# Moving small pieces of a tuned decoder trunk: first loads, three operands of the first SwiGLU, one raw sum, and the order of the last tiles

## The chip, the cores and the metric

The kernel runs on one core of a Trainium2 chip. Its time is the device time of one launch in microseconds (us); lower is better. The engines are named as in the profile: PE (TensorE, the matmuls, with PEld for its weight loads), DVE (VectorE), ACT (ScalarE), POOL (GpSimd) and SP (SyncE, which here only issues DMAs).

## The reference

Two layers over 512 tokens of width 1024, all in float32. Each layer is a SwiGLU block, a mixer (attention and a short convolution side by side) and a second SwiGLU block; a last RMSNorm ends it.

```python
def swiglu(h, w_gate, w_up, w_down):
    return (jax.nn.silu(h @ w_gate) * (h @ w_up)) @ w_down

for l in range(DEPTH):                       # DEPTH = 2, D_MODEL = 1024, D_FF = 2816
    x = x + 0.5 * swiglu(rms_norm(x, ffn1_norm[l]), ffn1_wg[l], ffn1_wu[l], ffn1_wd[l])
    h = rms_norm(x, mix_norm[l])
    z = h @ w_in[l]
    ...                                      # attention over 128 tokens, short convolution
    x = x + jnp.concatenate([attn_out, conv_out], axis=-1) @ w_out[l]
    x = x + 0.5 * swiglu(rms_norm(x, ffn2_norm[l]), ffn2_wg[l], ffn2_wu[l], ffn2_wd[l])
return rms_norm(x, final_norm)
```

## The kernel before

**Products.** Each float32 operand is split into a high part in fp32r and the rest (hi = cast on ACT, lo = raw - hi on DVE; `split`, L226), and a product takes three matmuls: hi x hi, hi x lo, lo x hi. Weights arrive as raw tiles of 512 KB (`load`, L209; eight buffers) and become `wh` and `wl`, three buffers each; `take_split` (L296) prepares them two groups ahead of PE.

**Seven products.** Most matrix products are done by a scheme of seven products in place of eight. The sums of the weights (`FORMS`: a11, a12, s2, s3, s1, a22, s4, each in two halves h = 0 and 1) are made partly by DMAs that accumulate (issued by POOL, L221: s1 and s3) and partly on DVE: s2 is the raw sum a11 + s1 (L265), made just before its split, and s4 is a12 + s2 (L285). The operands from the activations (`CHAINS`: b11, b21, t2, t3, t1, t4, b22) are made by `Seven.make`: t2, t1 and t4 need DVE subtractions or additions (L589 to L594), and all are split. In `winograd2` a loop over these seven steps streams one operand against one weight sum; steps are counted from 1 in the texts, so t2 is step 3, t1 step 5, t4 step 6, b22 step 7. A step is 24 matmuls of 128x512. After step n + 1 (n = 0, 1, 2) the operand of step n + 5 is made. The operands of a norm are made once and used by all its blocks, so this happens in the first block of a SwiGLU alone. Blocks are b = 1, 3, 5, 7, 9; b = 1 is the first, b = 3 the second.

**Order.** A planner (the tile framework) orders the instructions of each engine from its own costs; `tc.issue_after(ins)` puts what is traced inside it behind `ins` on that engine. Each engine then takes its instructions in that order. `state["rest"]` is the last lo split on DVE that was traced.

**Opening.** `x` comes token-major. `load_x(tp, c0, n)` loads columns c0 to c0 + n - 1 (of 128) of token half tp; `turn_x(c)` turns column tile c by four PE transposes, two from each token half, so it needs both halves' loads. `norm.take(c)` scales the turned tile into `xh` (ACT, L458) and `xl` (DVE, L459); `own` splits parts of the first three weight tiles, `go` multiplies them. `spin(n)` runs n matmuls on zeros. Order of the loads before: on ACT's queue x(0,1), then x(0,2) with x(0,3); on SP's queue x(0,0), x(1,0), half of the first weights, x(1,1), x(1,2) with x(1,3), the other half, and the rest.

**End.** The last seven-product block writes token-major. `close` adds a product to the output tile (DVE, L1318) and sums its squares (ACT, L1320); `guess` takes the reciprocal root (ACT, L1324) and `mend` refines it by one Newton step on DVE (L1329 for the mean, then three in `newton`, L433 to L435). `scale` multiplies half of the tile on DVE (L1364) and half on ACT (L1368) and issues the output DMA. The third token tile's product comes first, then the fourth's in two halves of 256 columns (`z_0`, `z_1`); in this section ACT and DVE run in the order in which the program is written.

## Time and profile before

| | |
|---|---|
| median of 3 runs | 1630.61 us (1630.34 to 1632.09) |
| the profiled execution | 1632.9 us, span 1631.1 us |
| PE busy | 1616.7 us, 99% of the span, 7572 matmuls |
| DVE busy | 1368.8 us, 84% |
| ACT busy | 1178.1 us, 72% |
| POOL busy | 223.6 us, 14% |
| granted PE clock, mean | 0.999 |

The span runs from the first instruction to the last; the rest of the execution's time lies around it. A row of the timeline gives the start in us from the start of the span, the duration, the engine (with q: its queue, which issues or waits), the line, the operation, the tile written and the tiles read, shapes and the count; in brackets the idle time of the engine before it and what ended it. A row of the waits gives the total, the times and the longest. A row of the critical chain gives start and length.

### The profile page before, as it was taken

The numbers are of one execution on the slowest core, as the hardware profiler recorded it, in microseconds if no ns is written. First come the engines' busy times: TensorE is split into PE (matmuls) and PEld (weight loads), VectorE is DVE, ScalarE is ACT, GpSimd is POOL, SyncE is SP. The second block draws the span as 40 slices with busy tenths as digits, with TensorE's granted clock in tenths as the row PEclk, the third lists the DMA queues.
The fourth block names the chain that finished last, engine by engine and source line by source line (L and its number), as shares of the span: only waits on it lengthen the run. The fifth ranks groups of instructions, "written<-read, shape, count | busy, mean of one in ns | idle before, by whom it ended". The sixth has DMA issues, their size and how long they took to land.

```text
span 1631.1 us, 21176 instructions
## 1 busy us (share of the span) xinstructions
PE 1616.7 (99%) x7572; PEld 1348.1 (83%) x7572; DVE 1368.8 (84%) x1779; ACT 1178.1 (72%) x1510; POOL 223.6 (14%) x199
## 2 busy tenths in 40 slices
PE   9999999999999999999999999999999999999998
PEld 6788888878898888888888888888788988888887
DVE  7978797888899977797999777989788998677997
ACT  6667777867766577778865777787586767878665
POOL 1211111001121111111011111110012111111121
PEclk9999999999999999999999999999999999999999
DMA  9899989922597698999967999999135978999992
GB/s 271 198 237 212 210 210 239 242 68 73 129 238 180 178 217 213 214 213 247 228 143 188 217 215 219 214 237 221 52 91 152 233 152 215 225 220 231 240 250 71
DMA packets 307166, 318.12 MB, mean 195 GB/s; under 512 B 125612, under 2 KB 188660, under 8 KB 307060
## 3 DMA queue, kind: packets, MB, share of 16 engines
q1 hardware_dynamic: 265140, 230.63, 49.9%
q0 software_dynamic: 41200, 85.47, 30.5%
q8 instruction: 59, 0.97, 0.2%
q10 hardware_dynamic: 720, 0.66, 0.1%
q14 instruction: 47, 0.39, 0.1%
HBM read 264.29 MB, written 2.10 MB: 163 GB/s over the span
## 4 chain that ended last, share of the span: by engine, by line
PE 91%; DVE 5%; ACT 2%; DMA 1%; issue 1%; SPq 0%; ACTq 0%; DVEq 0%
PE x L824 26%; PE y L824 13%; PE x_s L824 9%; PE w L824 6%; PE acc L313 6%; PE acc L312 6%; PE acc L315 6%; PE y_s L824 5%; PE w_s L824 3%; PE x_m L809 3%; PE y_m L809 1%; DVE wl L226 1%; PE y_e L824 1%; PE acc L686 1%; PE x_e L824 1%
## 5 line engine op out<-in xcount | busy, mean ns | idle before, releaser
L226 DVE TENSOR_TENSOR wl<-raw,wh 128x1024 fp32r<-128x1024 f32 (+1 forms) x493 | 599.6, 1224 | 171.8 <-ACT wh L226 171.0
L226 ACT CAST wh<-raw 128x1024 fp32r<-128x1024 f32 (+1 forms) x493 | 513.9, 1046 | 302.2 <-PE x L824 95.0
L313 PE MATMUL acc<-xl,wh 128*128 128x512 f32 x392 | 153.6, 392 | 2.8 <-DVE xl L459 2.8
L312 PE MATMUL acc<-xh,wh 128*128 128x512 f32 x392 | 153.4, 393 | 0.5 <-ACT wh L226 0.5
L315 PE MATMUL acc<-xh,wl 128*128 128x512 f32 x384 | 149.6, 390 | 0.0
L221 POOL DMA_DIRECT2D raw<-in_ffn_wu_dram x40 | 50.2, 1264 | 386.1 <-DVE wl L226 203.8
L313 PEld LDWEIGHTS acc<-xl,wh 128*128 128x128 f32 x392 | 73.7, 188 | 18.7 <-DVE xl L459 4.4
L312 PEld LDWEIGHTS acc<-xh,wh 128*128 128x128 f32 x392 | 73.7, 188 | 15.5 <-ACT wh L226 0.6
L315 PEld LDWEIGHTS acc<-xh,wl 128*128 128x128 f32 x384 | 72.1, 188 | 15.0
L221 POOL DMA_DIRECT2D raw<-in_ffn_wg_dram x40 | 49.4, 1261 | 200.9 <-DMA raw<-in_ffn_wu_dram 82.9
L221 POOL DMA_DIRECT2D raw<-in_ffn_wd_dram x34 | 41.0, 1206 | 246.3 <-DMA raw<-in_ffn_wd_dram 109.7
L265 DVE TENSOR_TENSOR raw<-raw,raw 128x1024 f32<-128x1024 f32 x58 | 70.6, 1221 | 3.6 <-DMA raw<-in_ffn_wu_dram 3.2
L1086 ACT COPY raw_a<-turned 128x1024 uint16<-128x1024 uint16 x48 | 63.5, 1357 | 0.0
L824 PE MATMUL x<-wl,ft2h 128*128 128x512 f32 x160 | 62.2, 390 | 1.1 <-DVE wl L226 1.1
L824 PE MATMUL y<-wh,ft4h 128*128 128x512 f32 x160 | 62.4, 390 | 0.1
L824 PE MATMUL w<-wh,fb21h 128*128 128x512 f32 x160 | 62.3, 390 | 0.0
L824 PE MATMUL y<-wh,ft3h 128*128 128x512 f32 x160 | 62.3, 390 | 0.0
L824 PE MATMUL w<-wl,fb21h 128*128 128x512 f32 x160 | 62.3, 389 | 0.0
L824 PE MATMUL x<-wh,ft2h 128*128 128x512 f32 x160 | 62.3, 389 | 0.0
L824 PE MATMUL x<-wh,ft1h 128*128 128x512 f32 x160 | 62.3, 389 | 0.0
L824 PE MATMUL x<-wh,ft2l 128*128 128x512 f32 x160 | 62.3, 389 | 0.0
L824 PE MATMUL x<-wh,ft1l 128*128 128x512 f32 x160 | 62.3, 389 | 0.0
(506 smaller groups left out, 4545.2 us busy)
## 6 DMA issues: line engine op xcount, KB each, us to landing
raw<-in_ffn_wu_dram SPq DMA_DIRECT2D x127, 512.0 KB, 5.4
raw<-in_ffn_wd_dram SPq DMA_DIRECT2D x105, 512.0 KB, 5.8
raw<-in_ffn_wg_dram SPq DMA_DIRECT2D x86, 512.0 KB, 5.3
raw<-in_ffn_wu_dram POOLq DMA_DIRECT2D x40, 512.0 KB, 8.9
raw<-in_ffn_wg_dram POOLq DMA_DIRECT2D x40, 512.0 KB, 6.2
raw<-in_w_in_dram SPq DMA_DIRECT2D x36, 512.0 KB, 4.0
raw<-in_ffn_wd_dram POOLq DMA_DIRECT2D x34, 512.0 KB, 9.4
raw<-raw POOLq DMA_DIRECT2D x21, 512.0 KB, 7.9
```

The lines of the kernel that those rows point to most:

```text
L221: nc.gpsimd.dma_start(out=r, in_=rows_of(*more), accum_op=ALU.add)
L226: return nc.scalar.copy(hi, raw), eng.tensor_sub(lo, raw, f32(hi))
L265: nc.vector.tensor_add(a11, a11, s1)
L312: nc.tensor.matmul(acc, hi[:, k, :], rhs[k][0], start=k == first, stop=False)
L313: nc.tensor.matmul(acc, hi[:, k, :], rhs[k][1], start=False, stop=False)
L315: nc.tensor.matmul(acc, lo[:, k, :], rhs[k][0], start=False, stop=k == last)
L686: nc.tensor.matmul(opening[n], (lo if part == "w" else hi)[:, k, :], xl if part == "x" else xh, start=n not in begun, stop=k == KC - 1 and ...
L809: nc.tensor.matmul(accs[c // 2][:, c % 2, :], w[:, k, cols], x_[:, 2 * h + k, :], start=start and c % 2 == 0 and h + k + i == 0, stop=h + ...
L824: nc.tensor.matmul(accs[u], x_[:, 2 * h + k, tok], w[:, k, :], start=start and h + k + i == 0, stop=h + k == 2 and i == 2, skip_group_chec ...
L1086: nc.scalar.copy(words(raws[self.b][:, c, :]), self.to[:, :, c, :])
```

## The change

1. The loads of x(1,1) and of x(0,2) with x(0,3) change queues and places. Two of the spins before the first transposes are left out.
2. In the first norm's SwiGLU (`norm.i == 0`) the operands of steps 5, 6 and 7 are made after steps 2, 3 and 4 instead of 1, 2 and 3, and their DVE instructions are put behind the last lo split traced by then.
3. In the first layer's first SwiGLU, block b = 3, the raw sum for the second half of s2 is put behind the lo split of the first half of a12 ("mark", "behind").
4. At the end `close` and `mend` are taken apart (`total` and `squared`, `mean` and `mend`), and the additions of the fourth token tile's two halves are written ahead of the scaling and of the small steps that wait for squares. The last Newton step takes two DVE instructions after the root instead of three, with one new small product ahead of it.

```diff
--- before.py
+++ after.py
@@ -261,6 +261,8 @@
                     late = state["late"] if h else None
                     if not state["late"] and how == "share":
                         late = state["rest"]
+                    if how == "behind":
+                        late = state["mark"]
                     with tc.issue_after(late) if late else nullcontext():
                         nc.vector.tensor_add(a11, a11, s1)
                 raw = {"a11": a11, "a12": a12, "s2": a11, "s3": s3, "s1": s1, "a22": a22, "s4": a12}[what]
@@ -271,6 +273,8 @@
                 sent = split_far(hi, lo, raw)
             else:
                 state["cast"], state["rest"] = (i.ins for i in split(hi, lo, raw))
+                if isinstance(order[n][1], tuple) and order[n][1][2] == "mark":
+                    state["mark"] = state["rest"]
             if isinstance(order[n][1], tuple) and order[n][1][0] == "end":
                 if what == "a12":
                     nc.gpsimd.dma_start(out=raw_of[raws["a11"]], in_=raw, accum_op=ALU.add)
@@ -383,7 +387,11 @@
                 if what == "w":
                     seven(
                         lambda o, j, h: ((wg, wu)[o], KC // 2 * j + 2 * h, 2, 2 * b * P, S),
-                        lambda what, h: "far" if (b, what, h) == (1, "a11", 0) else None,
+                        lambda what, h: "far"
+                        if (b, what, h) == (1, "a11", 0)
+                        else {("a12", 0): "mark", ("s2", 1): "behind"}.get((what, h))
+                        if near and b == 3
+                        else None,
                     )
                 if what == "s":
                     seven(
@@ -627,8 +635,8 @@
     load_x(1, 0, 1)
     load_x(0, 1, 1, nc.scalar)
     load(r0, 0, 0, 2)
-    load_x(0, 2, 2, nc.scalar)
-    load_x(1, 1, 1)
+    load_x(1, 1, 1, nc.scalar)
+    load_x(0, 2, 2)
     warm = small("warm", 1)
     nc.vector.memset(warm, 0.0)
     nc.scalar.activation(warm, warm, AF.Abs_reciprocal_sqrt, bias=eps)
@@ -716,7 +724,6 @@
     with tc.manual_schedule(engines={pe, act, dve}):
         spin(3)
         turn_rows(0)
-        spin(2)
         turn_x(0)
         own(0, 0, 2)
         norm.take(0, tps[0])
@@ -1015,8 +1022,10 @@
                             nc.scalar.activation(gates[2 + u], out, AF.Silu)
                             nc.vector.tensor_mul(ups[2 + u], ups[2 + u], gates[2 + u])
                 turns(step)
-                if step < 3:
-                    norm.make(CHAINS[step + 4][1])
+                due = step + (4 if norm.i else 3)
+                if 3 < due < len(CHAINS):
+                    with nullcontext() if norm.i else tc.issue_after(state["rest"]):
+                        norm.make(CHAINS[due][1])
                 if between:
                     between(step)
             if b in blocks:
@@ -1311,28 +1320,40 @@
             part = self.y[t][o]
             nc.vector.scalar_tensor_tensor(part, acc, by, part, op0=ALU.mult, op1=ALU.add)
 
+        def total(self, acc, t, half, by, c0=0):
+
+            y = self.y[t][half][:, c0 : c0 + acc.shape[1]]
+            nc.vector.scalar_tensor_tensor(y, acc, by, y, op0=ALU.mult, op1=ALU.add)
+            return y
+
+        def squared(self, y, ssq, name):
+
+            sq = work.tile([P, S], F32, tag="nsq", bufs=2, name=f"ysq_{name}")
+            nc.scalar.activation(sq[:, : y.shape[1]], y, AF.Square, accum_out=ssq)
+
         def close(self, acc, t, half, by, ssq, c0=0):
 
-            wide = acc.shape[1]
-            y = self.y[t][half][:, c0 : c0 + wide]
-            nc.vector.scalar_tensor_tensor(y, acc, by, y, op0=ALU.mult, op1=ALU.add)
-            sq = work.tile([P, S], F32, tag="nsq", bufs=2, name=f"ysq_{half}_{t}_{c0}")
-            nc.scalar.activation(sq[:, :wide], y, AF.Square, accum_out=ssq)
+            self.squared(self.total(acc, t, half, by, c0), ssq, f"{half}_{t}_{c0}")
 
         def guess(self, t, ssq, rest):
             r = small(f"r_end{t}", 1)
             nc.scalar.activation(r, ssq, AF.Abs_reciprocal_sqrt, scale=1.0 / D, bias=rest)
             return r
 
-        def mend(self, t, ssq, rest, r):
-            v, y = (small(f"{n}_end{t}", 1) for n in "vy")
+        def mean(self, t, ssq, rest):
+            v = small(f"v_end{t}", 1)
             nc.vector.scalar_tensor_tensor(v, ssq, 1.0 / D, rest, op0=ALU.mult, op1=ALU.add)
+            return v
+
+        def mend(self, t, v, r):
+            y = small(f"y_end{t}", 1)
             newton(y, r, v)
             return y
 
         def root(self, t, ssq, rest):
 
-            return self.mend(t, ssq, rest, self.guess(t, ssq, rest))
+            early = self.guess(t, ssq, rest)
+            return self.mend(t, self.mean(t, ssq, rest), early)
 
         def last(self, ops, accs):
 
@@ -1428,16 +1449,26 @@
             with tc.manual_schedule(engines={act, dve}):
                 ssq = piece(products(accs["x"][0], 0, 0, S, False), a, 0, 0.5)
                 early = self.guess(a, ssq, done[:, a : a + 1])
-                by = self.mend(a, ssq, done[:, a : a + 1], early)
+                v = self.mean(a, ssq, done[:, a : a + 1])
+                one = self.total(products(psum("mm", [P, H], "z_0"), 1, 0, H, True), b, 0, 0.5)
+                by = self.mend(a, v, early)
+                ssq = small("ssq_end_0", 1)
+                self.squared(one, ssq, "one")
                 for late in (0, 1):
                     scale(a, by, late)
-                one = piece(products(psum("mm", [P, H], "z_0"), 1, 0, H, True), b, 0, 0.5)
+                two = self.total(products(psum("mm", [P, H], "z_1"), 1, H, H, True), b, 0, 0.5, H)
                 rest = done[:, b : b + 1]
                 nc.vector.scalar_tensor_tensor(
-                    rest, one, 1.0 / D, rest, op0=ALU.mult, op1=ALU.add
+                    rest, ssq, 1.0 / D, rest, op0=ALU.mult, op1=ALU.add
                 )
-                two = piece(products(psum("mm", [P, H], "z_1"), 1, H, H, True), b, 0, 0.5, H)
-                by = self.mend(b, two, rest, self.guess(b, two, rest))
+                half = small("half", 1)
+                nc.vector.tensor_scalar_mul(half, rest, -0.5)
+                ssq, v, by = (small(f"{n}_last", 1) for n in ("ssq", "v", "y"))
+                self.squared(two, ssq, "two")
+                r = self.guess(b, ssq, rest)
+                nc.vector.scalar_tensor_tensor(v, ssq, -0.5 / D, half, op0=ALU.mult, op1=ALU.add)
+                nc.vector.tensor_scalar(v, v, r, r, op0=ALU.mult, op1=ALU.mult)
+                nc.vector.scalar_tensor_tensor(by, v, 1.5, r, op0=ALU.add, op1=ALU.mult)
                 for late in (1, 0):
                     scale(b, by, late)
```

## The prediction

> **What bounds the kernel now.** I read the page first, then the waits of the matmul engine, then the timeline at each place that the diff touches, and the critical chain there.
>
> ```profile
> span 1631.1 us, 21176 instructions
> PE 1616.7 (99%) x7572; PEld 1348.1 (83%) x7572; DVE 1368.8 (84%) x1779; ACT 1178.1 (72%) x1510; POOL 223.6 (14%) x199
> ```
> ```profile
> PE acc L313 <- DVE xl L459: 2.8, 4, 1.1
> PE xt L652 <- DMA xin<-in_x_dram: 1.6, 1, 1.6
> PE x L824 <- DVE wl L226: 1.1, 1, 1.1
> ```
>
> PE is busy 99% of the span. No matmul is added or removed except two spins, so the change can gain only where PE waits, and in the tail after its last matmul. The second view says how little that is: the three longest waits. The first (2.8) sits at the starts of the mixers, which the diff does not touch. The second is the opening, the third the first seven-product SwiGLU block. So the stakes are a few us of 1631; slower can come only from new waits.
>
> The profiled execution took 1632.9 us, 1.8 around the span; the median shown is 1630.61, or 2.3 less. I take the savings off the median. Differences under 0.2% (3.26 us) are about what a measurement of this kernel cannot tell from none.
>
> **Part 1, the opening.** Token tile 1 is turned from two loads; its second half, x(1,1), is what PE waits for.
>
> ```profile
> 1.21 0.98 ACTq L618 DMA_DIRECT2D xin<-in_x_dram  x2
> ```
> ```profile
> 2.30 4.59 DMA xin<-in_x_dram
> 11.45 3.24 PE acc L686 x13
> ```
> ```profile
> 1.19 2.74 PE L151 MATMUL idle<-zero 128*128 128x512 bf16 x6 [1.19 <-DVE warm L633]
> 4.08 0.61 PE L151 MATMUL idle<-zero 128*128 128x512 bf16 x2
> 6.93 0.44 PE L652 MATMUL xt<-ident,xin 128*128 128x128 f32 x2 [1.58 <-DMA xin<-in_x_dram]
> ```
> ```profile
> 5.64 0.40 ACT L226 CAST wh<-raw 128x256 fp32r<-128x256 f32 x1 [1.28 <-DMA raw<-in_ffn_wg_dram]
> 7.41 0.69 ACT L458 ACTIVATE xh<-xt,par 128x512 fp32r<-128x512 f32 x1 [0.78 <-PE xt L652]
> 8.46 0.42 ACT L226 CAST wh<-raw 128x256 fp32r<-128x256 f32 x1
> 9.92 0.69 ACT L458 ACTIVATE xh<-xt,par 128x512 fp32r<-128x512 f32 x1 [0.45 <-PE xt L652]
> ```
> ```profile
> DMA to landing us min/median/max: 4.6/4.7/4.9
> ```
>
> The first two fences show the exchange: x(1,1) is issued at 2.30 on SP's queue and lands at 6.89 (2.30 + 4.59, the chain's piece); x(0,2) with x(0,3) is the second of ACT's two, issued in the second half of their 0.98, about 1.7. They change places, so x(1,1) is issued 0.6 earlier and no longer behind 256 KB. It should land between 6.3 (0.6 earlier) and 5.6, where the first weights, issued beside it, have landed for the cast at 5.64. I take 5.6. ACT then goes from the first xh (ends 6.63) straight into the second (7.41): the 0.78 idle is gone. It does not all survive. The next cast, at 8.46, needs the second half of the first weights, issued at 3.33; the last row is the landing time of the two loads issued from 3.3 to 3.8, so 3.33 + 4.6 = 7.9. The bytes issued before it are the same, so the cast starts near 7.96: 0.50 gained, and the two xh behind it, the second of which (9.92) waits for PE, follow by 0.4 to 0.5. From 11.45 the chain is PE alone, so I carry **0.45** on. Ends: a loss of 0.15 (x(0,2) is issued 0.6 later and tile 2 waits for it: 0.45 less 0.6) and a gain of 1.2 (the weights come early too, so both the 0.78 and the 0.45 that ACT idles before the fourth xh go).
>
> The two spins (0.61) stood between a transpose group and a wait of 1.58 for data: free to remove, the cast at 5.64 waits for a DMA all the same.
>
> **Part 2, operands a step later.** In the first seven-product block VectorE is full. The first row is the busy time of the engines from 45 to 58 us, of 13.00 (PE, PEld, DVE, ACT, POOL, then the granted clock).
>
> ```profile
> 45.00:58.00 13.00, 12.12 (x54) 9.60 (x52) 13.00 (x12) 8.92 (x12) 3.69 (x5) 1.00 1.05 190
> ```
> ```profile
> 54.65 1.22 DVE L226 TENSOR_TENSOR ft1l<-hf,ft1h 128x1024 fp32r<-128x1024 f32 x1
> 56.92 1.22 DVE L226 TENSOR_TENSOR wl<-raw,wh 128x1024 fp32r<-128x1024 f32 x1
> 68.33 3.49 DVE L226 TENSOR_TENSOR wl<-raw,wh 128x1024 fp32r<-128x1024 f32 x3
> ```
> ```profile
> 96.08 5.44 PE x L824 x24
> ```
> ```profile
> 56.73 0.39 PE L824 MATMUL x<-wh,ft2l 128*128 128x512 f32 x1
> 58.19 0.50 PE L824 MATMUL x<-wl,ft2h 128*128 128x512 f32 x1 [1.07 <-DVE wl L226]
> 58.53 0.39 PE L824 MATMUL x<-wh,ft2h 128*128 128x512 f32 x1
> 68.98 0.39 PE L824 MATMUL x<-wh,ft1l 128*128 128x512 f32 x1
> 69.42 0.50 PE L824 MATMUL y<-wh,ft4h 128*128 128x512 f32 x1
> ```
>
> Step 3 (operand t2) runs four matmuls with wh, the last at 56.73, and gets its first wl at 58.14 (56.92 + 1.22). Undisturbed matmuls start 0.227 apart (the chain's 24 in 5.44), so it began near 56.04; 56.73 to 58.19 loses 1.23, and the next start, 0.34 on, another 0.11. Ahead of that wl stand the subtraction for t1 (L592) and ft1l, which step 5 needs only when it starts (four matmuls to 68.98, so 68.30). With the change they queue behind the last wl of s2. VectorE starts one every 1.14 (three in 3.49, the last taking 1.22), so two fewer bring the wl from 56.92 to about 54.7 (ScalarE's cast for it follows the raw sum at once), done at 55.9, before 56.5, when the third matmul wants it. That stall of 1.34 goes.
>
> What is late next is step 5. Its PE start moves from 68.30 to 66.96, so its first wl (68.33, the first of three) is wanted at 67.4. Of the work ahead of it fb22l (b22's) moves behind, now after s1's wl: done at 68.41 instead of 69.55. If ft4l, which now comes after s3's wl, falls behind as well, 67.27. So PE would be short by 0 to 1.0. Before, it was short by 1.25 and lost 0.32 (68.98 to 69.42 is 0.21 too long, and a restart of 0.11), because matmuls of the same and the next step were run in the gap. I take 0.2 lost where 0.32 was. ACT's three casts move along and issue no DMA. Part 2: 1.34 + 0.12 = **1.45**; ends 0.66 (1.0 paid where 0.32 was) and 1.66 (no stall left).
>
> **Part 3, the raw sum a part later.** The second block is where those gains could be taken back.
>
> ```profile
> 83.33 1.23 DVE L265 TENSOR_TENSOR raw<-raw,raw 128x1024 f32<-128x1024 f32 x1 [0.55 <-DMA raw<-in_ffn_wu_dram]
> 84.47 1.22 DVE L226 TENSOR_TENSOR wl<-raw,wh 128x1024 fp32r<-128x1024 f32 x1
> 87.78 1.23 DVE L265 TENSOR_TENSOR raw<-raw,raw 128x1024 f32<-128x1024 f32 x1 [1.49 <-DMA raw<-in_ffn_wu_dram]
> 89.53 1.22 DVE L226 TENSOR_TENSOR wl<-raw,wh 128x1024 fp32r<-128x1024 f32 x1
> ```
> ```profile
> 88.17 0.39 PE L824 MATMUL x<-wl,fb11h 128*128 128x512 f32 x1
> 90.88 0.42 PE L824 MATMUL w<-wl,fb21h 128*128 128x512 f32 x1
> ```
>
> VectorE takes its instructions in turn. The second raw sum waits 1.49 for an accumulating load, and queued behind it are a gate product and the wl at 89.53, done at 90.75; PE uses it at 90.88. So 0.13 of slack: the wait is just hidden. If PE comes 1.9 earlier (parts 1 and 2) and the load does not move, that order costs PE 1.8, nearly everything. With the change the sum stands behind this wl, which then follows its own cast, paced by PE's release of a buffer. The sum is wanted a step and a half (5.44 us each) later. So part 3 gains nothing by itself and keeps the gain: **0**. The first sum (83.33) is not moved; the wl behind it ends at 85.69, wanted at 88.17 now and 86.3 after: 0.6 of slack if its load stays where it is.
>
> **Part 4, the last tiles.**
>
> ```profile
> 1623.91 0.28 PE L1415 MATMUL z<-wl,fb_e 128*128 128x256 f32 x1
> 1623.04 0.75 DVE L1364 SCALAR_TENSOR_TENSOR ytok<-ytok,y_end,gain 128x512 f32<-128x512 f32 x1
> 1624.70 0.16 DVE L1436 SCALAR_TENSOR_TENSOR done<-ssq_end,done 128x1 f32<-128x1 f32 x1 [0.57 <-ACT ysq L1320]
> 1624.78 0.42 DVE L1318 SCALAR_TENSOR_TENSOR ytok<-z,ytok 128x256 f32<-128x256 f32 x1
> 1626.29 0.16 DVE L434 SCALAR_TENSOR_TENSOR v_end<-v_end,y_end 128x1 f32<-128x1 f32 x1
> 1626.49 0.16 DVE L435 SCALAR_TENSOR_TENSOR y_end<-v_end,r_end 128x1 f32<-128x1 f32 x1
> ```
>
> PE ends at 1624.19, but the last addition (L1318) starts at 1624.78: it stands behind L1436, which waits for the square of the first half. That came late because its addition stood behind the scaling at 1623.04. Now both additions go ahead, and the last can start near 1624.23: 0.55 earlier. After the root there are two small VectorE steps instead of three; one costs 0.19 (1626.29 to 1626.49). The new product with -0.5 (0.16) falls into the time of ScalarE's square. Sum **0.74**; ends 0.5 (the new order holds the last addition a little) and 0.8. The output DMA behind it is as before.
>
> **The sum.** 0.45 + 1.45 + 0 + 0.74 = 2.64: the profiled 1632.9 would be 1630.3, the median 1630.61 becomes 1628.0, 0.16% less. Ends of the parts together: 1.0 to 3.66, so 1629.6 to 1626.9.
>
> **Rivals.**
>
> *The opening gives its upper end.* If the weights land earlier together with x(1,1), ACT's two idle stretches go: 1.2 + 1.45 + 0.74 = 3.4, 1627.2, faster by just over 0.2%. For: the loads that share the queues change places. Against: no bytes go away. Chance 0.25.
>
> *The clock stays low.* Six spins took 2.74 (0.42 from start to start), the two later ones 0.61 (0.23): the clock rose at about 4. Without those two PE is emptier between 4 and 7; were it at half speed after that, each matmul that does not wait for anything else would cost 0.2 more, and as many as the chain's 13 from 11.45 would cost 2.6: no gain left, 1630.6. Against: it idled 1.58 before 6.93 and ran at 0.23 after. [...] Chance 0.05.
>
> *The new bound is step 5.* The full 1.0 is paid and x(0,2) is late: 1.0 gained, 1629.6. Chance 0.12.
>
> *Slower.* The first raw sum of the second block, still ahead of its wl, waits for a load that accumulates on the POOL queue.
>
> ```profile
> 74.69 1.21 POOL L221 DMA_DIRECT2D raw<-in_ffn_wu_dram  x1 [24.45 <-DVE wl L226]
> DMA to landing us min/median/max: 5.8/8.6/13.2
> ```
>
> That one was issued at 74.69 and landed by 83.3, 8.6 us; between 60 and 240 us such loads took 5.8 to 13.2. At 13.2 it lands 4.6 later; less 0.6 of slack PE stalls 4.0, and the kernel ends at 1632.0. It decides from a landing about 3.2 later than now, where the 2.64 are used up. For: the changed order moves the buffers' releases and so when these loads start and what they meet. Against: VectorE releases earlier, not later. Chance 0.10, most of it near the edge; with other new waits of the kind it holds the chance of slower by over 0.2%.
>
> **How the numbers follow.** The forecast holds 0.48, the rivals 0.25, 0.05, 0.12 and 0.10. Faster by over 0.2% is the first rival and the forecast's fast end: 0.31. Slower by over 0.2%: 0.09. The rest, 0.60, is within. The range goes from 1626.7 (the fast ends, and the 0.3 by which the fastest run lies under the median counted in part) to 1630.6 (no gain left); the forecast's own is 1627.3 to 1628.7.
>
> **What would show it.** In the changed profile: the wait of xt for xin under 0.5; no wait of x for wl near 56; ft1l behind the wl of s2; no VectorE wait for a raw in front of the wl at PE's w step near 88; the last addition within 0.1 of PE's end, and 0.74 less from there to the output DMA. Wrong, if PE shows a stall over 1 us between 60 and 90, or if the matmuls after 7 us start 0.42 apart.

## The result and the profile after

The change made the kernel 0.17% faster: the ratio of its time to that of before is 0.9983, interval 0.9975 to 0.9991 (22 runs each, medians 1631.07 and 1632.87 us). That is 2.8 us of 1633, with 1.5 and 4.1 as ends; the two medians themselves lie 1.8 apart. The forecast's saving (2.64 us, 0.16%) lies inside. Its level, 1628.0, and its range, 1626.7 to 1630.6, were too low: they stood on three runs with a median of 1630.61, while more runs put the kernel before at 1632.87 and the changed one at 1631.07. The profiled execution took 1632.4 us, against 1632.9 before, so this pair of profiles shows less of the saving than the times do.

The changed kernel's page (span, busy time) and its waits of PE (total, times, longest):

```profile
span 1630.6 us, 21172 instructions
PE 1617.5 (99%) x7570; PEld 1349.6 (83%) x7570; DVE 1367.9 (84%) x1779; ACT 1177.8 (72%) x1510; POOL 223.5 (14%) x199
```
```profile
PE acc L317 <- DVE xl L467: 2.8, 4, 1.1
PE xt L660 <- DMA xin<-in_x_dram: 1.2, 1, 1.2
PE idle L151 <- DVE warm L641: 1.2, 1, 1.2
PE acc L694 <- ACT xh L466: 0.8, 1, 0.8
```

The wait of x for wl (1.1 before) is gone. The wait for x(1,1) shrank from 1.6 to 1.2 only, and a new one of 0.8, for ACT, stands behind it in the opening. The largest, at the mixers, reads the same, but it isn't the same stalls (below).

To place time I use landmarks, each against its own place before: the first matmul of the fourth weight tile (28.67 us before, 30.20 after: the opening), the start of the first block's step 4, the start of the second block's step 4, PE's last matmul, and the last output DMA's issue. The first of these, before and then after:

```profile
28.67 0.50 PE L312 MATMUL acc<-xh,wh 128*128 128x512 f32 x1 [0.49 <-ACT wh L226]
30.20 0.50 PE L316 MATMUL acc<-xh,wh 128*128 128x512 f32 x1 [0.49 <-ACT wh L226]
```

| from, to | before, us | after, us | difference |
|---|---|---|---|
| start to fourth weight tile | 28.67 | 30.20 | +1.53 |
| to step 4, first block | 34.19 | 32.81 | -1.38 |
| to step 4, second block | 38.50 | 38.20 | -0.30 |
| to PE's end | 1522.83 | 1523.16 | +0.33 |
| to the last output's issue | 3.27 | 2.64 | -0.63 |

Parts 2 to 4 did what was forecast, nearly to the size. Part 1 cost 1.5 us in this execution, where 0.45 were forecast as gained. The sum of the rows is -0.45 to that issue, and -0.52 over the span.

**The opening.** PE, then ACT, of the changed kernel's timeline (start, us, then what ran, with the idle time ahead of it):

```profile
4.02 0.87 PE L660 MATMUL xt<-ident,xin 128*128 128x128 f32 x6
6.12 0.44 PE L660 MATMUL xt<-ident,xin 128*128 128x128 f32 x2 [1.22 <-DMA xin<-in_x_dram]
7.33 0.79 PE L694 MATMUL acc<-xh,wh 128*128 128x512 f32 x1 [0.77 <-ACT xh L466]
7.92 0.63 PE L694 MATMUL acc<-xh,wl 128*128 128x512 f32 x1
8.77 1.05 PE L660 MATMUL xt<-ident,xin 128*128 128x128 f32 x4
```
```profile
6.28 0.40 ACT L226 CAST wh<-raw 128x256 fp32r<-128x256 f32 x1 [1.98 <-DMA raw<-in_ffn_wg_dram]
6.59 1.26 ACT L466 ACTIVATE xh<-xt,par 128x512 fp32r<-128x512 f32 x2
```

x(1,1) lets PE go on at 6.12 instead of 6.93. But the first weights, whose cast ran at 5.64 before, land for 6.28, and ACT stands idle 1.98 for them. The four transposes at 8.77 take 1.05 us: such a group took 0.60 before (7.91). From 7.3 the clock is at half. The same in stretches of 3.41 us (the chip changed the granted clock at 3.90, 7.31 and 10.72 after, and at 4.13 before; columns: stretch, length, busy time of PE, PEld, DVE, ACT, POOL, granted clock, DMA share, GB/s). The changed kernel, then before:

```profile
0.49:3.90 3.41, 2.71 (x7) 0.77 (x7) 0.28 (x2) 1.58 (x2) 0.91 (x5) 1.00 0.53 155
3.90:7.31 3.41, 1.43 (x10) 0.93 (x9) 0.43 (x2) 1.20 (x4) 0.00 (x0) 1.00 0.92 276
7.31:10.72 3.41, 3.40 (x10) 2.70 (x11) 1.97 (x4) 2.12 (x4) 0.00 (x0) 0.50 1.06 351
```
```profile
4.13:7.54 3.41, 1.83 (x13) 1.33 (x13) 1.18 (x2) 1.30 (x4) 0.00 (x0) 1.00 0.96 287
7.54:10.96 3.42, 3.42 (x18) 2.26 (x17) 2.25 (x4) 2.97 (x6) 0.00 (x0) 1.00 1.04 352
```

In the middle stretch PE was busy 1.43 us of 3.41, and the next one ran at 0.50: ten matmuls in it where 18 ran before. Ahead of the first record the column prints 1.00; the pace there (six spins 0.42 apart, like the matmuls from 7.92 to 8.34 under a granted 0.50) says half.

**Steps 3 and 5.** VectorE and PE of the changed kernel:

```profile
56.20 1.22 DVE L226 TENSOR_TENSOR wl<-raw,wh 128x1024 fp32r<-128x1024 f32 x1
57.94 1.21 DVE L226 TENSOR_TENSOR wl<-raw,wh 128x1024 fp32r<-128x1024 f32 x1
59.67 1.22 DVE L600 TENSOR_TENSOR hf<-hf 128x1024 f32<-128x1024 f32 x1
63.07 1.22 DVE L226 TENSOR_TENSOR ft1l<-hf,ft1h 128x1024 fp32r<-128x1024 f32 x1
67.61 2.35 DVE L226 TENSOR_TENSOR wl<-raw,wh 128x1024 fp32r<-128x1024 f32 x2
```
```profile
57.80 0.39 PE L831 MATMUL x<-wh,ft2l 128*128 128x512 f32 x1
58.02 0.39 PE L831 MATMUL x<-wl,ft2h 128*128 128x512 f32 x1
68.90 0.49 PE L831 MATMUL x<-wl,ft1h 128*128 128x512 f32 x1
69.23 0.39 PE L831 MATMUL x<-wh,ft1h 128*128 128x512 f32 x1
```

The subtraction for t1 (59.67) and ft1l (63.07) stand behind the wl of s2. Step 3's third matmul (58.02) follows 0.22 behind the second. At step 5 PE takes its first wl at 68.90, just after it is made (the first of the two from 67.61, 1.22 long, ends at 68.83), and loses 0.10 once, at 69.23.

**The second block** in the changed kernel, VectorE and PE:

```profile
85.95 1.22 DVE L226 TENSOR_TENSOR wl<-raw,wh 128x1024 fp32r<-128x1024 f32 x1 [0.28 <-ACT wh L226]
87.69 1.22 DVE L267 TENSOR_TENSOR raw<-raw,raw 128x1024 f32<-128x1024 f32 x1
```
```profile
90.56 0.39 PE L831 MATMUL w<-wh,fb21l 128*128 128x512 f32 x1
90.78 0.39 PE L831 MATMUL w<-wl,fb21h 128*128 128x512 f32 x1
```

The wl comes at 85.95, before the raw sum, and is done 3.6 us before PE takes it (90.78).

**The end.**

```profile
1624.09 0.28 PE L1436 MATMUL z<-wl,fb_e 128*128 128x256 f32 x1
1624.40 0.42 DVE L1326 SCALAR_TENSOR_TENSOR ytok<-z,ytok 128x256 f32<-128x256 f32 x1 [0.41 <-PE z L1436]
1625.73 0.27 DVE L1470 TENSOR_SCALAR v_last<-v_last,r_end 128x1 f32<-128x1 f32 x1 [0.17 <-ACT r_end L1340]
1626.04 0.16 DVE L1471 SCALAR_TENSOR_TENSOR y_last<-v_last,r_end 128x1 f32<-128x1 f32 x1
1626.23 0.75 DVE L1385 SCALAR_TENSOR_TENSOR ytok<-ytok,y_last,gain 128x512 f32<-128x512 f32 x1
```

The last addition starts 0.03 after PE's end (1624.37), where it was 0.59. The first of the two remaining small steps takes 0.31 to the next start (1625.73 to 1626.04) where one of the old form took 0.19.

**What the pair of profiles hides.** Between the second block and PE's end the changed kernel has no edit, yet the two profiles drift by up to 2.2 us. Three times, near 316, 796 and 1121 us, ACT waits for a transposing DMA (turned), and the mixer's first matmuls stall when that wait is long. ACT, then PE, of before, then of the changed kernel:

```profile
316.17 2.57 ACT L911 COPY back<-turned 128x1024 uint16<-128x1024 uint16 x2 [3.50 <-DMA turned<-halves]
795.79 2.59 ACT L911 COPY back<-turned 128x1024 uint16<-128x1024 uint16 x2 [0.56 <-DMA turned<-halves]
```
```profile
341.75 0.50 PE L313 MATMUL acc<-xl,wh 128*128 128x512 f32 x1 [1.05 <-DVE xl L459]
```
```profile
313.75 2.60 ACT L918 COPY back<-turned 128x1024 uint16<-128x1024 uint16 x2 [1.24 <-DMA turned<-halves]
796.43 2.57 ACT L918 COPY back<-turned 128x1024 uint16<-128x1024 uint16 x2 [3.54 <-DMA turned<-halves]
```
```profile
821.97 0.50 PE L317 MATMUL acc<-xl,wh 128*128 128x512 f32 x1 [1.07 <-DVE xl L467]
```

Before, the first place waits 3.50 and PE stalls at 341.75; the second waits 0.56 and costs nothing. After, it is the other way round. At the third place both wait (3.38 and 3.13) and PE stalls in both. So one profile of each kernel weighs the edits only through landmarks near them, and the time only through many runs.

### The profile page after: what moved, and what is told of

Its sections match the earlier page's. It is cut to its first block, busy times and chain, and to the rows that moved or that the text cites. A ratio compares the mean times of both kernels' runs of the same rounds, so it can differ in the third digit from the quotient of the medians.

```text
span 1630.6 us, 21172 instructions
## 1 busy us (share of the span) xinstructions
PE 1617.5 (99%) x7570; PEld 1349.6 (83%) x7570; DVE 1367.9 (84%) x1779; ACT 1177.8 (72%) x1510; POOL 223.5 (14%) x199
## 4 chain that ended last, share of the span: by engine, by line
PE 94%; DVE 3%; ACT 1%; DMA 1%; issue 1%; ACTq 0%; DVEq 0%
PE x L831 27%; PE y L831 13%; PE x_s L831 9%; PE w L831 7%; PE acc L317 6%; PE acc L316 6%; PE acc L319 6%; PE y_s L831 5%; PE x_m L816 3%; PE w_s L831 3%; PE y_m L816 1%; PE y_e L831 1%; PE acc L694 1%; PE x_e L831 1%; DVE wl L226 1%; PE w_m L816 1%
## 5 line engine op out<-in xcount | busy, mean ns | idle before, releaser
L831 PE MATMUL x<-wl,ft1h 128*128 128x512 f32 x160 | 62.4, 390 | 0.0
L831 PE MATMUL x<-wh,fb11l 128*128 128x512 f32 x160 | 62.3, 389 | 0.0
L831 PE MATMUL x<-wh,fb11h 128*128 128x512 f32 x160 | 62.3, 389 | 0.0
L831 PE MATMUL y<-wh,ft3l 128*128 128x512 f32 x160 | 62.3, 389 | 0.0
L831 PE MATMUL x<-wl,fb11h 128*128 128x512 f32 x160 | 62.3, 389 | 0.0
```

The costliest lines, as they stand in the source:

```text
L831: nc.tensor.matmul(accs[u], x_[:, 2 * h + k, tok], w[:, k, :], start=start and h + k + i == 0, stop=h + k == 2 and i == 2, skip_group_chec ...
```

## The experiments

The edits are of four kinds: the loads, the spins, the operands with the raw sum, the end. Each kernel has one or some of them. Each ratio is to the kernel before, timed beside it, from 12 executions of the experiment (7 of e10). The landmarks come from one profiled execution of each kernel, and are given against those of before.

**e1_spins_back**: the changed kernel with the two spins.

```diff
         turn_rows(0)
+        spin(2)
         turn_x(0)
```

> The changed kernel with the two spins of the opening put back; loads, operands, raw sum and end stay changed. Marker of the opening: start of the first matmul behind it that takes xh and wh of the fourth weight tile (28.67 us in the profile of before, 30.20 in that of the changed kernel). Clock theory: the opening lost 1.5 us because PE was too empty between 4 and 7 us without the spins and its clock fell to half for 3.4 us; with them it does not fall, matmuls after 7 us start 0.23 apart, marker 28.2 to 28.7. Load theory: the loss comes from the exchange of the loads, which let the first half of the first weights land at 6.26 instead of 5.62; the spins change nothing, marker at 29.3 or later with the clock full. Time: by the clock theory 0.1% below the changed kernel where its clock falls, 0.2% below the kernel before; by the load theory 0.12% below before.

Measured: 0.9983 (0.9972 to 0.9995). The clock is full from 5.86, the first cast is at 6.74, the fourth tile's first matmul at 29.45, and the opening costs 0.78 instead of 1.53. From there on the landmarks are those of the changed kernel: -1.38 to step 4, -1.71 in all to the second block, 2.65 at the end. Each theory holds in half: the clock stays full, and the landmark is where the load theory put it. So with the clock up, the late weights alone still cost 0.8 here. The half clock is worth at least the 0.75 between the two kernels, as the weights were later in this one (6.74 against 6.28). In the time the difference can't be seen.

**e3_spins_out**: the kernel before without them.

```diff
         turn_rows(0)
-        spin(2)
         turn_x(0)
```

> The kernel before without the two spins, all else as before. Clock theory: the clock falls to half near 7 us for 3.4 us in those executions whose count of PE's work ends badly, and the marker goes from 28.67 to 29.5 to 30.5; granted clock over the run 0.998 in more of the executions than the 0.999 of before. Load theory: nothing happens, marker 28.5 to 28.8, time as before within 0.1%.

Measured: 1.0005 (0.9990 to 1.0021). The first cast is at 6.15 and the clock stays at half until 10.61. PE of e3:

```profile
7.20 0.80 PE L686 MATMUL acc<-xh,wh 128*128 128x512 f32 x1
8.64 1.06 PE L652 MATMUL xt<-ident,xin 128*128 128x128 f32 x4
```

The fourth tile's first matmul comes at 30.13, 1.46 late. With the loads unmoved, the spins' absence alone gives the pace of the changed kernel's opening. The mean granted clock is 0.998 or less in 5 of its 12 executions and in 7 of the 35 of before beside them, as the clock theory said. The time shows no difference outside its interval.

**e8_without_opening**: the changed kernel with the old loads and the spins.

```diff
-    load_x(1, 1, 1, nc.scalar)
-    load_x(0, 2, 2)
+    load_x(0, 2, 2, nc.scalar)
+    load_x(1, 1, 1)
...
         turn_rows(0)
+        spin(2)
         turn_x(0)
```

> The changed kernel with loads and spins of the opening as before; operands, raw sum and end stay changed. If the parts add up, marker 28.67 as before, no stall of PE at the first wl of step 3, from PE's end to the last output DMA 0.7 less: 1.6 + 0.7 = 2.3 us less than before, 0.14%. If the opening as changed is a gain in most executions and the fallen clock rare, this one is 0.3 us slower than the changed kernel; if the clock falls mostly, 1 us faster.

Measured: 0.9984 (0.9969 to 0.9999). Cast at 5.67, full clock from 4.09, fourth tile at 28.35, then -1.43, and -1.75 in all to the second block, and 2.65 at the end. All the saving that the time shows is there without part 1, though the interval is wide.

**e4_operands_only**: part 2 on the kernel before.

```diff
-                if step < 3:
-                    norm.make(CHAINS[step + 4][1])
+                due = step + (4 if norm.i else 3)
+                if 3 < due < len(CHAINS):
+                    with nullcontext() if norm.i else tc.issue_after(state["rest"]):
+                        norm.make(CHAINS[due][1])
```

> The kernel before with part 2 alone: the operands of steps 5 to 7 a step later, the raw sum of the second block where it was. Theory of the cover: the stall of 1.34 us at step 3 and that of 0.32 near 69 us go, but VectorE's wait for the accumulating load (1.49 us at 87.78) is no longer hidden and PE stalls near 88 us by 0.5 to 1.8 us, so by 93 us the gain is 0 to 1.1 us. Rival: the load comes earlier as PE and VectorE do, PE does not stall there and 1.6 us stay without the moved raw sum, which is then worth nothing.

Measured: 0.9986 (0.9973 to 1.0000). -1.40 to step 4, but only -0.83 in all to the second block's: part of the gain is paid back there. VectorE, then PE, of e4:

```profile
86.73 1.23 DVE L265 TENSOR_TENSOR raw<-raw,raw 128x1024 f32<-128x1024 f32 x1 [1.13 <-DMA raw<-in_ffn_wu_dram]
88.47 1.22 DVE L226 TENSOR_TENSOR wl<-raw,wh 128x1024 fp32r<-128x1024 f32 x1
```
```profile
89.74 0.50 PE L824 MATMUL w<-wl,fb21h 128*128 128x512 f32 x1 [0.57 <-DVE wl L226]
```

The raw sum waits 1.13 for its accumulating load, the wl stands behind it, done at 89.69, and PE takes it at 89.74 after idling 0.57.

**e5_operands_and_sum**: e4 with the raw sum moved (a part of the edit).

```diff
...
+                    if how == "behind":
+                        late = state["mark"]
                     with tc.issue_after(late) if late else nullcontext():
                         nc.vector.tensor_add(a11, a11, s1)
...
```

> The kernel before with parts 2 and 3: operands a step later and the second raw sum behind a wl. With the operands alone, PE stalled 0.73 us at 89.7 behind VectorE's wait for the load, and of 1.7 us gained against its own marker by 61 us 0.8 was left at 100 us. Theory of the cover: here no stall near 89 us, and 1.7 us less from the marker to the fourth step of the second block (72.69 us in before). Rival: that stall was an accident of one landing; then this kernel has the same 1.7 with or without the moved sum, and VectorE shows no wait over 0.3 us for a raw between 80 and 92 us.

Measured: 0.9989 (0.9975 to 1.0003). -1.40 to step 4 and -1.70 to the second block, no stall near 89. Part 3 keeps 0.87 of part 2 (1.70 - 0.83), in these two executions. The other kernels agree: between 45 and 300 us, PE idles for over 0.1 us once in each of the four profiles without part 2 (1.05 to 1.08, at step 3), once in e4 (the 0.57 above), and not at all in the eight with parts 2 and 3. The first cast of e5 came at 6.73 with the loads of before: a late landing isn't the new loads' alone.

**e2_loads_only**: the kernel before with the new loads and its two spins.

```diff
-    load_x(0, 2, 2, nc.scalar)
-    load_x(1, 1, 1)
+    load_x(1, 1, 1, nc.scalar)
+    load_x(0, 2, 2)
```

> The kernel before with the exchanged loads alone, spins kept. The changed kernel with its spins back had its marker (start of the first matmul of the fourth weight tile) at 29.45, against 28.67, 28.35 and 28.46 in three kernels with the old order, and its first cast of weights at 6.74 against 5.64, 5.67 and 5.58. If the exchange does that: first cast at 6.2 to 6.8, marker 29.2 to 29.6, 0.05% slower than before. If it was scatter of one execution: first cast at 5.6, marker 28.2 to 28.7, as forecast in the prediction (0.45 less).

Measured: 0.9996 (0.9983 to 1.0009). Cast at 6.52; the clock fell at 7.59 and rose at 11.01 though both spins were there, and the fourth tile came at 30.47, 1.80 late. Two stretches of e2:

```profile
4.18:7.59 3.41, 1.65 (x11) 0.97 (x10) 0.47 (x2) 1.24 (x4) 0.00 (x0) 1.00 0.96 291
7.59:11.01 3.42, 3.42 (x10) 2.67 (x11) 1.98 (x4) 2.08 (x4) 0.00 (x0) 0.50 1.05 360
```

The cast is where the first theory put it; the landmark is 0.87 beyond its range, with the clock at half. So two spins don't secure the clock: e1 has the same opening and kept it. Here it fell after a stretch with PE busy 1.65, and it stayed up in before after 1.83.

**e6_end_only**: part 4 on the kernel before (the diff's last two hunks alone).

```diff
+                one = self.total(products(psum("mm", [P, H], "z_0"), 1, 0, H, True), b, 0, 0.5)
                 by = self.mend(a, v, early)
...
+                two = self.total(products(psum("mm", [P, H], "z_1"), 1, H, H, True), b, 0, 0.5, H)
```

> The kernel before with part 4 alone. From PE's last matmul end to the issue of the last output DMA: 3.27 us before, 2.62 to 2.65 in the three kernels with the new end so far; here 2.6 to 2.7, everything ahead as before, so 0.6 us less (0.04%), which the times of the runs cannot tell from nothing.

Measured: 1.0000 (0.9984 to 1.0016); 2.65 from PE's end to the last output, as in every kernel with the new end (2.64 to 2.65), against 3.26 to 3.27 with the old one (before, e2 to e5): 0.62. Its profiled span is 1625.9, 5.2 under that of before, while its time is the same: this execution has none of the mixers' stalls. Its page:

```profile
span 1625.9 us, 21179 instructions
```

**e7_more_spins**: e8 with eight more spins. (The texts written before the runs count nine; four, two, one and one are eight, and PE has 7580 matmuls for 7572.)

```diff
         turn_x(0)
+        spin(4)
         own(0, 0, 2)
...
             turn_x(c)
+            spin(2 if c == 1 else 1)
```

> The changed kernel with loads and spins of the opening as before, and nine spins more in PE's waits there: four behind the first transposes, two behind the second, one behind each of the third and fourth. Clock theory, carried on: executions that are 4 to 8 us longer than the fastest are those in which PE's clock is at half in parts of the opening; with PE kept busy there the clock stays full from about 5 us, the marker is 28.2 to 28.7, no execution has a granted clock of 0.998 or less, and the median falls by 1 to 2 us under that of the same kernel without them (1629.1). Rival: the spins only delay what PE has to do, marker 29 or later, same scatter; then the scatter has another cause, such as the landing of the transposing DMAs that ScalarE waits for at 316, 796 and 1121 us.

Measured: 0.9978 (0.9966 to 0.9990). Cast at 6.14, full clock from 6.81, fourth tile at 29.50: 0.83 later than before in this execution, and yet the lowest ratio so far. The first theory misses: the full clock came at 6.81 and not near 5, the landmark is late as the rival said, and one of the 12 executions still has a mean granted clock of 0.998. Its median, 1630.03, was taken beside a kernel before at 1633.21, and e8's 1629.13 beside one at 1632.44.

**e10_new_loads_spins**: e7 with the changed kernel's loads.

> The changed kernel's loads with the two spins back and nine more, and parts 2 to 4. If the changed opening loses to two things, the first weights' landing (about 0.8 us) and a clock at half for 3.4 us (about 0.8), the spins take away the second alone: full clock from 6.9 on, first cast 6.3 to 6.7, first matmul of the fourth weight tile at 29.4 to 29.6; ratio 0.998. Rival: the order of the loads alone sets the opening, the clock costs nothing: that matmul at 30.2 with full clock, ratio 0.9985.

Measured: 0.9977 (0.9966 to 0.9987), from 7 executions. Cast at 6.35, full clock from 6.91, fourth tile at 29.55. The first theory holds: with the clock up, what is left is 0.88. But the spins are in the way too. PE of e10:

```profile
5.76 1.60 PE L151 MATMUL idle<-zero 128*128 128x512 bf16 x4
7.20 0.60 PE L660 MATMUL xt<-ident,xin 128*128 128x128 f32 x4
```

The second column tile's transposes start at 7.20, behind the four spins and without any wait for data.

**e9_weights_on_act**: e7, with the first weights as ACT's third load and x(1,1) as SP's third (a part of the edit).

```diff
-    load(r0, 0, 0, 2)
-    load_x(0, 2, 2, nc.scalar)
     load_x(1, 1, 1)
+    load(r0, 0, 0, 2, nc.scalar)
+    load_x(0, 2, 2)
...
```

> Parts 2 to 4, the first half of the first weights as third load of ACT's queue, x(1,1) as third of SP's with x(0,2) behind it, and nine more spins. If a load lands by its place in its queue, the first cast stays at or before 5.7 us and the second token half no longer waits, so the first matmul of the fourth weight tile comes near 28.0 (28.7 before, 30.2 changed); ratio near 0.9975. Rival: what lands first is a matter of shared bandwidth, not of places: first cast 6.2 to 6.7, that matmul at 29.4, ratio 0.998 to 0.9985. The clock should be full from 6.9 at the latest in both.

Measured: 0.9988 (0.9975 to 1.0002). Cast at 5.98, fourth tile at 29.66 with full clock from 7.22. Both expectations miss the landing, which is between them, and the rival is nearer on the opening: it gains nothing, since here too the spins hold the second column tile's transposes, to 7.35. This order shows no gain over e7's. Its execution lost the clock once more, far from the opening. Two stretches of e9:

```profile
823.01:826.42 3.41, 1.98 (x8) 0.84 (x6) 3.41 (x6) 2.01 (x4) 0.00 (x0) 1.00 0.25 46
826.42:829.83 3.41, 3.41 (x8) 2.66 (x9) 2.37 (x3) 2.86 (x3) 0.00 (x0) 0.50 0.28 108
```

These are the mixer's first matmuls behind the second transposing DMA, for which ACT waited 3.23. PE waited 1.4 in all for xl, was busy 1.98 in the stretch, and ran the next at half clock; in e7 that piece of time holds 17 matmuls instead of 8.

**e11_changed_again**: the changed kernel.

> The changed kernel again. If its opening is set by its order: first cast 6.2 to 6.8, clock at half for one count of 3.4 us before 11, first matmul of the fourth weight tile at 30.0 to 30.5, then the start of step 4 at -1.4 and of the second block's at -1.7 against it, and 2.64 us from PE's end to the last output. Rival: the landing and the clock's count fall out by chance, so one of them is away: 29.4 or below. Ratio 0.998 in both.

Measured: 0.9983 (0.9970 to 0.9997), as in the result above. The first cast is at 5.89 this time, and no wait for x(1,1) is left, but the clock stays at half until 10.37: the fourth tile comes at 29.89. -1.38 and -1.71 behind it, and 2.65 at the end. So the landing does scatter, as the rival had it; the half clock was there again, and the place was 0.1 outside the range of the first theory.

## Why the prediction was right, and where it was not

**Part 1 failed**, in sign: +1.53 and +1.22 in the two profiles of the changed kernel, where -0.45 was said and +0.15 was the worst end. Two steps of it fell. Two of the prediction's own signs show it: the wait of xt for xin is 1.2 and not under 0.5, and matmuls after 7 us start 0.42 apart (7.92 and 8.34), which it had named as a sign of being wrong. The signs for the other parts came as listed, but for 0.63 in place of 0.74 at the end.

*The bytes issued before it are the same, so the cast starts near 7.96.* This, like the first cast left at 5.64, took the landing of the first weights for fixed. In the changed kernel their casts came at 6.28 and 8.57, where 5.64 and 7.96 were reckoned with. The openings:

| kernel | loads, spins | first cast | clock at half | fourth tile |
|---|---|---|---|---|
| before | old, 2 | 5.64 | to 4.13 | 28.67 |
| e8 | old, 2 | 5.67 | to 4.09 | 28.35 |
| e4 | old, 2 | 5.58 | to 6.62 | 28.46 |
| e6 | old, 2 | 5.49 | to 6.34 | 28.45 |
| e5 | old, 2 | 6.73 | to 6.77 | 29.43 |
| e1 | new, 2 | 6.74 | to 5.86 | 29.45 |
| e2 | new, 2 | 6.52 | to 4.18; 7.59 to 11.01 | 30.47 |
| e3 | old, none | 6.15 | to 10.61 | 30.13 |
| after | new, none | 6.28 | to 3.90; 7.31 to 10.72 | 30.20 |
| e11 | new, none | 5.89 | to 10.37 | 29.89 |
| e7, e10, e9 | old, new, e9's; 10 | 6.14, 6.35, 5.98 | to 6.81, 6.91, 7.22 | 29.50, 29.55, 29.66 |

With the new loads the first cast came at 5.89 to 6.74 (five kernels, mean 6.36), with the old ones at 5.49 to 6.73 (seven, mean 5.91). Whether x(1,1) takes its time from the weights is not shown: in e5 both were late (PE went on at 7.00, the cast came at 6.73), in e4 and e6 neither was. With the clock up, an opening with a cast before 5.7 ends near 28.5, one with a cast near 6.7 at 29.4: about 1 us. The ranges overlap, so "the new loads land the weights later" is likely, and not shown.

*The two spins: free to remove.* Every wait around them was for data, but they kept PE busy. Without them three of three profiled executions ran at half clock between 7.4 and 10.3, with the two spins one of seven (e2), with ten none of three. The rival that says so had 0.05 and a price of up to 2.6. An estimate of the price goes by the openings with two spins and the clock up: 28.48 for a cast at 5.60 (the mean of before, e8, e4 and e6) and 29.44 for one at 6.74 (e5 and e1). On the line through these, the four openings at half clock would have come at 28.7 (e11) to 29.3 (e2), and each came 1.1 to 1.2 later. By this estimate most of the opening's loss in the changed kernel is the clock's, and 0.1 to 0.4 is that of the weights.

The prediction's argument against, that PE idled 1.58 before 6.93 and ran at 0.23 after, weighed a single gap. Where the clock changed more than once at the start (after, e2), the changes lie 3.41 us apart; in e9 the fall at 826.42 lies 819.20, or 240 such stretches of 3.413, behind the rise at 7.22. The "count" in the texts of e3 and e11 is taken here as such a stretch. Counted off in such stretches from the changes that each kernel's records show, PE's busy time in a stretch (the union of its matmuls, ends as the profile models them) and the clock of the next are ("end" is the stretch with PE's last matmul):

| clock in the stretch | busy of 3.41 us | clock in the next |
|---|---|---|
| full | 0.48 (e7, end), 1.23 (e2, end), 1.43 (after), 1.65 (e2), 1.98 (e9, at 823.01) | half |
| full | 1.57 (e1, end), 1.72 (e9, end), 1.83 (before), 2.14 (before, end), 2.20 (e1), 2.42 (e8) | full |
| half | 2.35 (e11), 2.59 (e3), 2.62 (e9), 2.52 (e11), 2.77 (e3) | half |
| half | 2.71 (after), 2.90 (e8), 2.94 (before), 2.99 (e2), 3.03 (e5) | full |
| half | 3.41 (e1, e4, e6, e7, e9, e10) | full |

In these stretches the clock fell from full after each one with PE busy 1.43 us or less, and after none with 2.14 or more. Between these it did both: it fell after 1.65 and 1.98 and stayed after 1.57, 1.72 and 1.83. From half it rose after each with 2.90 or more and after none with 2.62 or less; between these it rose after 2.71 and stayed at half after 2.77. Whether anything beside PE's busy time counts was not tried. The longest pause in the changed kernel's stretch was a wait of 1.22, shorter than the one of 1.58 after which before kept its clock. The stretches begin at different times in different executions (3.90 in after, 4.13 in before). Of two kernels with the same opening e1, whose first change lies at 5.86, kept the clock after it, and e2, whose first lies at 4.18, lost it at 7.59.

**Part 2 was right, and undersized.** The stall of 1.34 at step 3 went as worked out: -1.38, and the same -1.37 to -1.43 in every kernel with the part. The bound that was to follow, step 5, cost 0.10 where 0.2 was taken: PE got its wl at 68.90 with 0.07 to spare, as ft4l fell behind too (69.89), the faster of the two cases that were weighed. The shortage before was misread there: 1.25 counts from the step's start (68.30), while the 1.0 set beside it counts from the third matmul; counted so, before was short by 0.80 (69.55 against 68.75). With the second block -1.68 stands against -1.45, at the end of the range given (1.66).

**Part 3 was right.** In e4, with PE 1.62 earlier than before at step 4, the load that the raw sum waits for came only 1.05 earlier (86.73 against 87.78), the wl was late, and 0.87 of the gain was lost. The prediction's bound for this, with a load that does not move, was 1.8; the load moved in part. The slower rival, the same wait at the first raw sum, cost nothing. The changed kernel has no wait there (82.71); e1, e5 and e7 wait 0.7 to 1.8 and e4 1.73, and PE does not stall behind it in any of them.

**Part 4 was right, and oversized.** 0.56 at the last addition (0.55 said), but 0.07 instead of 0.19 behind the root: two small steps for three, of which the new one, with two scalars read from tiles, takes 0.31 instead of 0.19. Together 0.62 for 0.74.

**The sum.** By the landmarks -1.7 and -0.62 against +1.2 to +1.5: -0.8 to -1.1. The times say -2.8, with -1.5 as the near end. So the total agrees with the forecast of -2.64 better than its own parts do, and part of this agreement is luck. The opening's loss, so plain in the profiles, doesn't show in the times: without part 1 (e8) the ratio is 0.9984, with it 0.9983. These intervals cannot exclude it, as 1.2 us are 0.0007.

Why the times say more than the landmarks stays open. Parts 2 and 3 show no saving elsewhere: from the second block's step 4 to PE's end the eight kernels with both take 1522.2 us on the mean, and the four with neither 1520.8, the mixers' stalls included. The kernel before loses time to the opening or the clock in some executions too. e5, with its opening, had a late landing. Its own mean granted clock was 0.998 or less in 24 of the 95 executions timed beside the experiments, and these are 2.4 us longer on the mean than the other 71; for the changed kernel it is 12 of 34, and 0.8 us. Two of the profiled executions have 0.998 (after, e2), and both lost the clock. In the unprofiled ones the record doesn't say where, and e9 shows that it need not be the opening.

The kernels with all of parts 2 to 4 stand at 0.9977 to 0.9988, and each interval holds 0.9985, so none can be called better than the changed kernel. e10 and e7 have the lowest ratios, but what their spins bring (0.0006 against e11 and e8) is less than half of an interval.

## What to carry to other kernels

Before taking filler work off an idle matmul engine, add up its busy time in the profile, in stretches as long as the changes of the granted clock lie apart there (3.41 us here), and not the single gaps: here the clock fell to half after every stretch at full clock with 1.43 us of work or less and after some with up to 1.98, and matmuls then started 0.42 apart instead of 0.23. When two small loads are exchanged at the start, ask which of the ones beside them pays: here PE's wait for x(1,1) fell from 1.6 to 1.2, while the first cast of the weights went from 5.64 to 6.28. And when an engine in order is relieved at one place, follow the gain to the next instruction that waits for a transfer, as the raw sum here did (1.13 in e4, where 0.87 of the gain was lost), and move that too.

## What the runs showed of the hardware

Three waits for transposing DMAs, in a part of the kernel that no edit touches, took between nothing and 3.7 us in different executions, and PE's waits behind them between 0 and 1.4 us in all at each place. At the first place a wait up to 1.4 cost PE nothing in the 13 profiles, and one of 2.4 to 3.7 cost it 0.3 to 1.4. In e9 the clock fell to 0.50 at 826.42, behind the second place. e6's execution had none of those stalls and a span of 1625.9; before's had them at two of the three places and 1631.1. Where this scatter comes from was not tried.

A VectorE step on 128x1 with both factors as scalars from tiles took 0.27, and 0.31 to the next start, against 0.16 and 0.19 for the form that it replaced.
